# Moving two groups of tiles by 64 and 128 bytes within the 256-byte grid of on-chip memory

## The chip, the cores and the metric

The kernel runs on one core of one Trainium2 chip. The metric is the device time of one execution in microseconds (us). The profile is of one execution on the same kind of core. In it PE is TensorE's matmul, PEld is TensorE's loading of the stationary operand, DVE is VectorE, ACT is ScalarE, POOL is GpSimd and SP is SyncE. Both operands of a matmul lie in the on-chip memory, SBUF, which has 128 partitions; every tile here has one address, which is its byte offset in each of the partitions it spans.

## The reference

A decoder trunk for one sequence of 256 tokens and width 1024, in two layers. Each layer has two half-step SwiGLU feed-forward blocks (inner width 2816) around a mixer. The mixer of the first layer is a short gated convolution, that of the second is sparse attention (16 heads of 64) over one shared key and value set, which is projected from the stream between the layers.

```python
def rmsnorm(x, g):
    y = x * lax.rsqrt(jnp.mean(x * x, axis=-1, keepdims=True) + EPS)
    return y * g

def swiglu_ffn(x, w_in, w_out):
    gate, up = jnp.split(x @ w_in, 2, axis=-1)
    return (jax.nn.silu(gate) * up) @ w_out

def short_conv_mixer(x, w_in, conv_w, w_out):
    b_gate, c_gate, v = jnp.split(x @ w_in, 3, axis=-1)
    y = causal_depthwise_conv(c_gate * v, conv_w)        # width 3
    return (b_gate * y) @ w_out

for i in range(2):
    if i == 1:
        kv = shared_kv(h, ...)                           # x @ w_kv, compression, key norms
    h = h + 0.5 * swiglu_ffn(rmsnorm(h, ffn1_norm[i]), ffn1_w_in[i], ffn1_w_out[i])
    hn = rmsnorm(h, mix_norm[i])
    h = h + (short_conv_mixer(hn, ...) if i == 0 else nsa_mixer(hn, ..., kv))
    h = h + 0.5 * swiglu_ffn(rmsnorm(h, ffn2_norm[i]), ffn2_w_in[i], ffn2_w_out[i])
```

Almost all the arithmetic is in the matrix products with weights.

## The kernel before, in words

**Numbers in two halves.** TensorE multiplies here in a rounded 32-bit format. So that little is lost, each factor is split into a high part (the rounded value, written by ScalarE) and a low part (the remainder, written by VectorE). A product is high by high, low by high and high by low, three matmuls' worth of columns. An activation tile holds [high | low], 256 columns of each, 2048 bytes per partition. One matmul with the high weight as the stationary operand streams all 512 columns past it, and one with the low weight streams the 256 high columns. That is `half` (its matmul is the line that the profile calls L497), which the passes `a_pass`, `a_group`, `ffn_in` and `out_proj` call for nearly everything.

**Weights.** `W` brings weights from memory into staging tiles `ws` by SyncE's queue, ScalarE rounds them into `wh` (L260, L183), VectorE writes the remainder into `wl` (L288, L194); there are six buffers of 4096 bytes of each. `W.take` and `W.done` hand them to the matmuls in a fixed order and set how far ahead conversion may go. The order of instructions on each engine is written out by hand; no planner rearranges it.

**Pairs.** Three of the four feed-forward output projections go through `Blocks.product` (L843), within `inner_pairs` (about 131 to 181 us and 402 to 452 us) and the last one (about 900 to 955 us). There the hidden tiles are the stationary operand (128 columns of act, pr, hm, and a few of xs, kt or t2) and 512 columns of wh or wl stream past them. Other places where weights stream: the kv projection (L1085 to L1087, L1146) and the query projection `q_step` (L1420 to L1422, 256 columns, xs stationary). At L475, in the norm's row sums, the stationary tile is all ones.

**Where tiles lie.** `mk(shape, tag, bufs)` takes a tile from a pool in which each tag has `bufs` buffers of the size of its largest tile. The tags lie one behind the other in the order in which they are first used. In the kernel before, byte offsets in a partition are:

| tag | what | first address | buffers x bytes | address modulo 256 |
|---|---|---|---|---|
| ones | constant for the norm's sums | 640 | 1 | 128 |
| ws | staged weights | 29216 | 3 x 8192 | 32 |
| xs | normed activations | 53792 | 8 x 2048 | 32 |
| kt | attention keys, squares | 71200 | 1 x 8192 | 32 |
| wh, wl | high and low weights | 79392, 103968 | 6 x 4096 each | 32 |
| t2, t1 | temporaries | 128544, 142880 | 7 x 2048, 6 x 1024 | 32 |
| u | convolution input | 151072 | 2 x 1088 | 32 (the second 96) |
| act | hidden activations, high and low | 153248 | 22 x 2048 | 160 |
| pr, hm | hidden tiles of the pairs, attention's tiles | 198304, 216736 | 6 x 3072, 5 x 2048 | 160 |

Slices of these tiles that a matmul takes begin at multiples of 512 or 1024 bytes behind the tile's start, so a slice has the same address modulo 256 as its tile.

The tag "u" is first used in `Pairs.room`, whose tile of T + 16 = 272 numbers (T = 256) gives it 1088 bytes. Only T numbers of it are used there; the convolution (`conv_evac`) later takes tiles of T + 2.

Of the kernel before, what the change touches and what calls it, by code (L numbers as in the profile page):

```python
# [16 lines left out]
P = 128  # L17
T = 256
# [44 lines left out]
def trunk(ctx, tc, A, out):  # L63
# [9 lines left out]
    uid = [0]  # L73

    def mk(shape, tag, bufs, dt=F32, pool=None):
        uid[0] += 1
        return (pool or sb).tile(list(shape), dt, tag=tag, name=f"{tag}_{uid[0]}", bufs=bufs)
# [16 lines left out]
    def t1(shape=(P, T)):  # L94
        return mk(shape, "t1", 6)

    def sm(shape):
        return mk(shape, "sm", 24)


    class Halves:
        def __init__(self):
# [9 lines left out]
    class Stream:  # L112
# [110 lines left out]
        def room(self):  # L223
            i = len(self.units) + len(self.half)
            if i >= min(len(self.where), self.cap):
                return False
            return i in self.spare or i - sum(s < i for s in self.spare) < self.freed + self.limit
# [177 lines left out]
    def new_xs():  # L405
        return [mk([P, 512], "xs", 8, F32R) for _ in range(8)]
# [150 lines left out]
    class Pairs:  # L557
# [4 lines left out]
            self.homes, self.plain, self.f, self.left, self.both, self.n = homes, plain, [], [], None, 0  # L562

        def room(self):
            return mk([P, T + 16], "u", 2)[:, :T] if len(self.f) < 2 and 0 not in self.plain else t1()

        def parts(self, h, l, src):
            ac.copy(h, src)
# [151 lines left out]
        W.pump(1 if n == 8 else NBUF)  # L720


    xs = new_xs()
    nm = Norm([(xs, G_FFN1)])

    sq_all = mk([P, 4, 2, T], "kt", 1)
# [1126 lines left out]
```

## Time and profile before

| what | value |
|---|---|
| time, median of 3 runs | 963.18 us (962.69 to 963.33) |
| the profiled execution's own time | 962.88 us |
| its span, first to last instruction | 961.1 us |
| mean granted TensorE clock | 1.00 of full speed |
| busy: PE, PEld, DVE, ACT, POOL | 955.8, 827.2, 815.2, 618.0, 145.7 us |
| DMA read from memory | 175.52 MB, 184 GB/s over the span |

Busy times count an engine's instructions; PE and PEld overlap, and matmuls overlap each other in the pipeline, so a matmul's own duration (some 390 ns for 512 columns) is longer than the time from its start to the next one's. The group rows read: line, engine, operation, output <- inputs (the moving operand first or second, by name), sizes, count, then busy us and mean ns of one. Timeline rows read: start us, length us, engine, line, operation, output <- inputs, sizes, count of instructions that are run together in the row.

### The profile page before, as it was taken

The page shows a single profiled execution, that of the slowest core. Times are in us where ns is not written, and L with a number is a line of the kernel's source. Part 1 is how long each engine was busy: PE and PEld are TensorE (multiplying, and loading weights), DVE is VectorE, ACT ScalarE, POOL GpSimd, SP SyncE. Part 2 cuts the span into 40 slices and gives each one's busy share as a digit, 9 for nine tenths or more (in the row PEclk, how much of TensorE's full clock was granted, in tenths as well). Part 3 has the DMA queues.
Part 4 walks back from the last instruction along what each step waited for, and adds up shares of the span by engine and source line. Part 5 has one row for each costly group of instructions (what it writes and reads, how often), then busy time and mean ns, then how long its engine had stood idle before and what let it go on. Part 6 is the DMA issues. An engine that isn't in the chain of part 4 may idle for free.

```text
span 961.1 us, 14541 instructions
## 1 busy us (share of the span) xinstructions
PE 955.8 (99%) x5425; PEld 827.2 (86%) x5425; DVE 815.2 (85%) x1352; ACT 618.0 (64%) x1056; POOL 145.7 (15%) x231
## 2 busy tenths in 40 slices
PE   9999999999999999999999999999999999999998
PEld 7888888888888888888888898888987888888887
DVE  7898899898899888999968887865589788878996
ACT  7666665665556665666858777744589656656653
POOL 1000000024460000000021042002237350000002
PEclk9999999999999999999999999999999999999999
DMA  8665743464546567463536866554520354467361
GB/s 303 225 225 176 275 160 136 176 218 166 187 146 250 186 209 264 130 219 139 212 132 194 265 223 238 190 205 148 211 89 2 132 220 155 156 222 254 133 191 71
DMA packets 42150, 178.59 MB, mean 186 GB/s; under 512 B 3776, under 2 KB 7504, under 8 KB 27104
## 3 DMA queue, kind: packets, MB, share of 16 engines
q1 hardware_dynamic: 42080, 177.67, 54.1%
q8 instruction: 42, 0.69, 0.3%
q14 instruction: 28, 0.23, 0.1%
HBM read 175.52 MB, written 1.08 MB: 184 GB/s over the span
## 4 chain that ended last, share of the span: by engine, by line
PE 97%; DVE 1%; ACT 1%; DMA 0%; issue 0%
PE mm L497 55%; PE a L497 13%; PE a L843 12%; PE mm L843 6%; PE a L1146 1%; PE mm L750 1%; PE mm L1499 1%; PE a L1569 1%; PE a L1544 1%; PE a L789 1%; DVE pr L1507 0%; PE a L1239 0%; PE mm L752 0%; PE a L1085 0%; PE a L1087 0%; PE a L1086 0%
## 5 line engine op out<-in xcount | busy, mean ns | idle before, releaser
L497 PE MATMUL mm<-xs,wh 128*128 128x512 f32 x1480 | 349.0, 390 | 0.0
L497 PEld LDWEIGHTS mm<-xs,wh 128*128 128x128 f32 x1480 | 273.7, 188 | 54.4 <-DVE xs L452 0.2
L288 DVE TENSOR_TENSOR wl<-ws,wh 128x1024 fp32r<-128x1024 f32 x217 | 271.2, 1259 | 28.4 <-ACT wh L260 18.7
L260 ACT CAST wh<-ws 128x1024 fp32r<-128x1024 f32 x217 | 224.7, 1045 | 15.3 <-PE a L497 7.5
L497 PEld LDWEIGHTS mm<-xs,wl 128*128 128x128 f32 x1480 | 185.2, 191 | 4.2
L497 PE MATMUL mm<-xs,wl 128*128 128x256 f32 x1480 | 187.3, 283 | 0.0
L516 DVE TENSOR_TENSOR t<-mm,t 128x512 f32<-128x512 f32 x95 | 65.1, 685 | 37.8 <-ACT t L515 37.1
L515 ACT COPY t<-mm 128x512 f32<-128x512 f32 x95 | 55.4, 584 | 41.4 <-PE mm L497 40.9
L843 PE MATMUL a<-wh,act 128*128 128x512 f32 x286 | 78.2, 395 | 0.0
L843 PEld LDWEIGHTS a<-wh,act 128*128 128x128 f32 x286 | 53.7, 188 | 12.3
L540 ACT ACTIVATE t<-t 128x256 f32<-128x256 f32 x84 | 35.1, 418 | 43.7 <-DVE t L527 43.5
L497 PE MATMUL a<-act,wh 128*128 128x512 f32 x256 | 61.4, 395 | 0.0
L497 PEld LDWEIGHTS a<-act,wh 128*128 128x128 f32 x256 | 47.5, 188 | 10.6
L509 ACT CAST act<-t 128x256 fp32r<-128x256 f32 x77 | 31.3, 407 | 28.8 <-DVE t L966 18.5
L416 ACT ACTIVATE xs<-base 128x256 fp32r<-128x256 f32 x32 | 16.1, 508 | 50.4 <-DVE base L659 35.5
L527 DVE TENSOR_TENSOR t<-t,R 128x256 f32<-128x256 f32 (+1 forms) x88 | 45.0, 511 | 2.7
L194 DVE TENSOR_TENSOR wl<-base,wh 128x1024 fp32r<-128x1024 f32 x39 | 46.6, 1221 | 0.0
L843 PE MATMUL a<-wl,act 128*128 128x512 f32 x143 | 44.7, 394 | 0.0
L194 DVE TENSOR_TENSOR wl<-ws,wh 128x1024 fp32r<-128x1024 f32 x32 | 38.1, 1221 | 1.0 <-ACT wh L183 1.0
L541 DVE TENSOR_TENSOR t<-t,t 128x256 f32<-128x256 f32 x84 | 35.3, 420 | 2.9 <-ACT t L540 2.9
L510 DVE TENSOR_TENSOR act<-t,act 128x256 fp32r<-128x256 f32 x77 | 33.7, 438 | 4.3 <-ACT act L509 4.3
L183 ACT CAST wh<-base 128x1024 fp32r<-128x1024 f32 x32 | 32.5, 1044 | 6.7 <-DVE base L189 5.5
(379 smaller groups left out, 1435.5 us busy)
## 6 DMA issues: line engine op xcount, KB each, us to landing
ws<-in_ffn_w_in_dram SPq DMA_DIRECT2D x69, 1024.0 KB, 4.9
base<-in_ffn_w_pairs_dram SPq DMA_DIRECT2D x32, 512.0 KB, 5.2
ws<-in_ffn_w_pairs_dram SPq DMA_DIRECT2D x26, 512.0 KB, 4.8
ws<-in_conv_w_in_dram SPq DMA_DIRECT2D x12, 1024.0 KB, 4.8
ws<-in_ffn_w_out_dram SPq DMA_DIRECT2D x11, 1024.0 KB, 4.8
base<-in_ffn_w_in_dram SPq DMA_DIRECT2D x11, 1024.0 KB, 5.3
ws<-in_w_kv_dram SPq DMA_DIRECT2D x6, 1024.0 KB, 5.0
kt<-in_ffn_w_in_dram SPq DMA_DIRECT2D x5, 1024.0 KB, 8.3
```

The source lines that it names most:

```text
L183: ac.copy(h, src)
L194: ve.tensor_tensor(out=l, in0=src, in1=h.bitcast(F32), op=ALU.subtract)
L260: ac.copy(h, src)
L288: ve.tensor_tensor(out=l, in0=src, in1=h.bitcast(F32), op=ALU.subtract)
L497: pe.matmul(o if x == 0 else o[:, :T], u[x][:, q * P:(q + 1) * P], rhs if x == 0 else rhs[:, :T], start=start, stop=stop, skip_group_check ...
L510: ve.tensor_tensor(out=dst[:, T:], in0=src, in1=dst[:, :T].bitcast(F32), op=ALU.subtract)
L515: ac.copy(r, o[:, :, T:])
L516: ve.tensor_tensor(out=r, in0=o[:, :, :T], in1=r, op=ALU.add)
L527: ve.tensor_tensor(out=r, in0=r, in1=R[:, None, :].to_broadcast([P, n, T]), op=ALU.mult)
L540: ac.activation(s, r[:, 0], AF.Silu)
L541: ve.tensor_tensor(out=s, in0=s, in1=r[:, 1], op=ALU.mult)
L843: pe.matmul(self.m[n], x, w, start=(c == 0), stop=(c == 3 * self.total[n] - 1), skip_group_check=True)
```

## The change

A helper `gap(n)` takes a tile of n bytes that nothing uses, under a tag of its own. A gap of 64 bytes is taken just before the first xs tile, and one of 192 just after. The tag "u" grows from 1088 to 1152 bytes per buffer, of which there are two. No instruction is added, removed or reordered.

```diff
+    def gap(n):
+        mk([P, n // 4], f"gap{uid[0]}", 1)
...
         def room(self):
-            return mk([P, T + 16], "u", 2)[:, :T] if len(self.f) < 2 and 0 not in self.plain else t1()
+            return mk([P, T + 32], "u", 2)[:, :T] if len(self.f) < 2 and 0 not in self.plain else t1()
...
+    gap(64)
     xs = new_xs()
+    gap(192)
     nm = Norm([(xs, G_FFN1)])
```

By the table's sizes, xs comes to lie at 96 modulo 256; kt, wh, wl, t2, t1 and the first u stay at 32; and act, pr and hm come to lie at 32, since two times 1152 is a multiple of 256. 384 bytes per partition more are taken.

## The prediction

> **What bounds the kernel now.** I read the page first: the busy shares, the granted clock, the chain that ended last.
>
> ```profile
> span 961.1 us, 14541 instructions
> PE 955.8 (99%) x5425; PEld 827.2 (86%) x5425; DVE 815.2 (85%) x1352; ACT 618.0 (64%) x1056; POOL 145.7 (15%) x231
> PEclk9999999999999999999999999999999999999999
> PE 97%; DVE 1%; ACT 1%; DMA 0%; issue 0%
> L497 PE MATMUL mm<-xs,wh 128*128 128x512 f32 x1480 | 349.0, 390 | 0.0
> L497 PE MATMUL mm<-xs,wl 128*128 128x256 f32 x1480 | 187.3, 283 | 0.0
> L843 PE MATMUL a<-wh,act 128*128 128x512 f32 x286 | 78.2, 395 | 0.0
> ```
>
> TensorE is busy 99% of the span at full clock, and 97% of the chain is its own. No wait can be taken away, and the change adds no instruction. Only the time from one matmul's start to the next can move. A single matmul's mean (390 ns) is no measure of that, because matmuls overlap in the pipeline. I take the pace from the timeline instead: a run's start subtracted from the next run's start, divided by the run's count.
>
> **What the change moves.** Nothing but addresses. The weight tiles (wh, wl) and xs start at 32 modulo 256 before, and act, pr and hm at 160, because two convolution buffers of 1088 bytes make 2176, that is 8 x 256 + 128. Two of 1152 make 9 x 256, so act, pr and hm drop to 32, where weights lie. The 64 bytes ahead of xs put it at 96, and the 192 bytes behind it put the rest back at 32. Write "distance" for the start of the stationary operand less the start of the moving one, modulo 256. Three kinds of matmul change theirs: (a) act, pr or hm with wh or wl goes from 128 (half a turn) to 0; (b) xs moving through wh or wl goes from 0 to minus 64 (a quarter turn); (c) the few with xs as the stationary side, or xs beside pr and hm, get plus or minus 64.
>
> **Does the distance show in the trace?** Distance 0 first, xs moving through weights (start, length, count):
>
> ```profile
> 26.19 7.44 PE L497 MATMUL mm<-xs,wh 128*128 128x512 f32 x32
> 33.47 4.00 PE L497 MATMUL mm<-xs,wl 128*128 128x256 f32 x32
> 37.30 4.95 PE L497 MATMUL mm<-xs,wh 128*128 128x512 f32 x21
> ```
>
> (33.47 - 26.19) / 32 = 227.5 ns for 512 columns, and (37.30 - 33.47) / 32 = 119.7 ns for 256. Now half a turn, act moving through the same weights at the same line:
>
> ```profile
> 622.86 5.06 PE L497 MATMUL a<-act,wh 128*128 128x512 f32 x21
> 627.75 2.77 PE L497 MATMUL a<-act,wl 128*128 128x256 f32 x22
> 630.36 5.53 PE L497 MATMUL a<-act,wh 128*128 128x512 f32 x23
> 635.72 5.39 PE L497 MATMUL a<-act,wl 128*128 128x256 f32 x44
> 640.94 10.38 PE L497 MATMUL a<-act,wh 128*128 128x512 f32 x44
> 651.16 5.45 PE L497 MATMUL a<-act,wl 128*128 128x256 f32 x44
> 656.45 10.43 PE L497 MATMUL a<-act,wh 128*128 128x512 f32 x44
> ```
>
> 512 columns: 4.89/21 = 232.9, 5.36/23 = 233.0, 10.22/44 = 232.3. 256 columns: 2.61/22 = 118.6, 5.22/44 = 118.6, 5.29/44 = 120.2. So half a turn costs some 5.5 ns on 512 columns and saves up to 1 ns on 256. The same with weights as the moving side, at L843, half a turn:
>
> ```profile
> 139.63 2.03 PE L843 MATMUL a<-wh,act 128*128 128x512 f32 x8
> ...
> 146.61 0.62 PE L843 MATMUL a<-xs,pr 128*128 128x512 f32 x2
> ```
>
> 30 matmuls start between these rows: 6.98/30 = 232.7. With weights moving at distance 0 (the kv projection, its stationary side kt or t at 32):
>
> ```profile
> 477.81 0.39 PE L1086 MATMUL a<-wh,t 128*128 128x512 f32 x1
> ...
> 482.34 1.07 PE L497 MATMUL a<-kt,wh 128*128 128x512 f32 x4
> ```
>
> 20 matmuls, 4.53/20 = 226.5. It follows the distance and not the operand that moves: both orders give 227 at 0 and 232.5 at 128.
>
> **The cost of each part.** The counts:
>
> ```profile
> 0.00:961.10 961.10, 170.38 (x729) 137.19 (x729) 1.00 0.54 186
> L497 PE MATMUL a<-act,wh x256: 387/393/404, 255.8 to 770.3; 128*128 128x512 f32 x128
> L497 PE MATMUL mm<-act,wh x32: 387/393/476, 746.2 to 765.5; 128*128 128x512 f32 x32
> L497 PE MATMUL a<-xs,wh x56: 389/389/389, 204.0 to 255.6; 128*128 128x512 f32 x56
> L843 PE MATMUL a<-xs,hm x18: 390/393/404, 161.9 to 946.2; 128*128 128x512 f32 x18
> L843 PE MATMUL a<-xs,pr x15: 390/392/404, 146.6 to 917.6; 128*128 128x512 f32 x15
> L843 PE MATMUL a<-xs,act x3: 390/390/392, 169.8 to 945.9; 128*128 128x512 f32 x3
> L843 PE MATMUL a<-act,hm x6: 396/397/397, 132.7 to 404.2; 128*128 128x512 f32 x6
> ```
>
> (The first is the window view of L843 alone: 729 matmuls.)
> - L843 to distance 0: 729 less 36 with xs and 6 that keep their distance (act with hm) is 687; x (232.7 - 227.0) = minus 3.9 us.
> - L497, act moving, 512 columns: 288 x (232.7 - 227.5) = minus 1.5 us.
> - L497, act moving, 256 columns: 288 x (119.7 - 118.9) = plus 0.2 us (up to 0.3).
> - The attention's small matmuls on act, pr and hm: some 300, bounded by the same 6 ns, plus or minus 1.8 us; taken as nil, being of other widths with no pair of rows to compare.
> - The two gaps issue no instruction. Nothing is queued or waits: 0.
>
> Together minus 5.2, rounded down to 5.1 us, if VectorE and ScalarE keep up. This cover is thin where most of L843 stands:
>
> ```profile
> 131.00:181.00 50.00, 50.00 (x216) 40.50 (x215) 48.40 (x53) 32.38 (x43) 0.00 (x0) 1.00 0.48 168
> 402.50:452.00 49.50, 49.50 (x215) 40.12 (x214) 48.00 (x53) 32.37 (x43) 0.00 (x0) 1.00 0.50 170
> 901.00:947.00 46.00, 46.00 (x199) 37.29 (x199) 43.58 (x47) 29.45 (x38) 1.91 (x2) 1.00 0.48 160
> 24.00:127.00 103.00, 103.00 (x600) 91.45 (x599) 92.03 (x158) 67.63 (x106) 0.00 (x0) 1.00 0.65 220
> ```
>
> (PE busy, PEld, VectorE, ScalarE, POOL.) In the first window PE would need 216 x 5.7 = 1.2 us less: 48.8 us against VectorE's 48.4. It still fits, by 0.4.
>
> The Trainium skill speaks against all of this: "SBUF — State Buffer", section "Who interferes with whom", gives TensorE two independent read ports, one for the moving operand and one for LDWEIGHTS, and names the port pair of VectorE and GpSimd as the only contention. By that rule no address matters to a matmul, and the sum would be 0. The rows at 227.5 and 232.7 do not agree with it.
>
> **The large unknown is (b).** xs moving through weights is 1480 + 56 (L497) and 48 more (L750, L789) of each width: 1584 of 512 columns and 1584 of 256. No row has a stationary operand 64 below the moving one. Bounds:
> - Below: the pace at distance 0 has a part that does not grow with the columns. 227.5 - 119.7 = 107.8 ns for 256 columns, so 119.7 - 107.8 = 11.9 ns is fixed. Distance 128 leaves 118.6 - (232.7 - 118.6) = 4.5 by the same reckoning, so part of it depends on addresses. If a quarter turn removed all of it, 3168 x 11.9 = minus 37.7 us.
> - Above: half a turn's price, 1584 x 5.5 = plus 8.7 us. The dearest single row is longer: 404 ns at half a turn against 389 at distance 0, so 1584 x 15 = plus 23.8 us if every one were such.
>
> The nearest row of another distance than 0 and 128 is the norm's matmul, its stationary tile of ones at 128 against a moving t at 32 (plus 96):
>
> ```profile
> 487.00 1.07 PE L497 MATMUL a<-t,wh 128*128 128x512 f32 x4
> 487.91 1.07 PE L497 MATMUL a<-kt,wh 128*128 128x512 f32 x4
> 492.57 1.07 PE L497 MATMUL a<-t,wh 128*128 128x512 f32 x4
> 493.48 0.40 PE L475 MATMUL a<-t,ones 128*128 128x256 f32 x2
> ```
>
> The four ahead of it take 0.91/4 = 227.5 ns, as four with weights behind them do (0.91/4). So loading weights from another quarter shows neither gain nor loss. It is one load, and no steady stream of them. I take nil for (b), keep both ends for the range, and leave (c), under 230 matmuls, inside them.
>
> **The forecast.** The profiled execution took 962.9 us: 961.1 of span and 1.8 around it. 962.9 - 5.1 = 957.8. The median is 963.18, 0.3 above the profiled execution; from it the same gain gives 958.1. I say 958.
>
> **Rivals.**
> 1. *A quarter turn takes part of the fixed 11.9 ns.* For it: that part is left even where matmuls queue back to back, and half a turn changes it. Against it: the row of ones shows no gain. Half of it gives 19 us: 963.2 - 5.1 - 18.9 = 939. The Trainium skill bears on the floor: "TensorE: Matmul & The Clock Gate", section "Step-by-step: what each phase is for", says that loading the next tile's weights takes no read bandwidth from the running matmul; 512 columns at one per cycle of the 2.4 GHz it states would be 213.3 ns, an estimate, and the trace's 227.5 stays above it.
> 2. *A quarter turn costs like half a turn, or more: slower.* Its place is L497 with xs moving, over half of the span (1584 x 347 ns = 550 us). With 5.5 ns on each of 1584: 963.2 - 5.1 + 8.7 = 966.8; with 15 ns, 982. It decides from 5.1 us / 1584 = 3.2 ns per matmul of 512 columns. For it: the one other distance that the trace shows in a steady stream is dearer than 0, and VectorE's 92.03 of 103 us shows nothing else that could hold xs's stages. Against it: the row of ones.
> 3. *Addresses do not matter, or tiles do not land where the change's words say.* 963. It would need the 5.5 ns to belong to the stage rather than the distance. Against it: L497 shows both paces with the same weights, and L843 and L1086 both with weights moving. This is also what the first rule of the Trainium skill above would give.
> 4. *VectorE becomes the bound at L843.* With half the gain lost there and in the out-projections: minus 2 to 3 us, 960.5. For it: 48.40 of 50 us busy. Against it: 0.4 us of room.
>
> **How the numbers follow.** This kernel's runs tell a difference from none at about 0.2%, 1.9 us. Forecast 0.34; rival 1 0.24; rival 2 0.28; rival 3 0.08; rival 4 0.06. Faster: 0.34 + 0.24 + 0.04 of rival 4 = 0.62. Slower: 0.24 of rival 2. Same: the other 0.04 of rival 2 (near its break-even), 0.08 and 0.02 of rival 4 = 0.14. The likeliest case's own range is 955 to 960. Both signs hold much of the chance, so the whole range goes from 936 (rival 1 at a bit over half) to 972 (rival 2 with 9 ns on each).
>
> **What would show it.** In the changed kernel's rows, the medians of L497 with act moving fall from 393 to 389 ns, those of L843 from 392 to 389, and the 44-matmul runs from 10.22 to 10.0 us. The 32-matmul run of xs stays at 7.28 us if (b) is nil; 7.46 is rival 2, 7.1 or less rival 1. VectorE's busy time in 131 to 181 us stays at 48.4 while PE's stage shortens by 1.2 us; idle time of PE before L843, released by VectorE, would be rival 4. Paces of act unchanged at 232.7 would be rival 3 and break the sum. A span above 965 or below 950 would say that (b), taken as nil, was the larger term.

## The result, and the profile after

The changed kernel takes 955.56 us (median of 5 runs, 955.45 to 956.31) against 963.18 (962.69 to 963.33): a ratio of 0.9924, with a 95% interval of 0.9911 to 0.9938. That is 7.6 us faster, where 5.1 were forecast. One execution among the experiments below (all tiles 32 bytes on) took 1913.45 us at the full granted clock, twice as long as the others of its kernel, and is left out of that kernel's median. The changed kernel's profiled execution took 955.53 us, 953.7 of it span. From the page of the changed kernel:

```profile
span 953.7 us, 14541 instructions
PE 947.8 (99%) x5425; PEld 819.0 (86%) x5425; DVE 814.9 (85%) x1352; ACT 617.7 (65%) x1056; POOL 144.8 (15%) x231
PE 85%; DVE 9%; ACT 2%; issue 2%; POOL 1%; DMA 0%; SPq 0%; ACTq 0%; DVEq 0%
L500 PE MATMUL mm<-xs,wh 128*128 128x512 f32 x1480 | 351.2, 392 | 0.2 <-DVE xs L423 0.2
L500 PE MATMUL mm<-xs,wl 128*128 128x256 f32 x1480 | 181.4, 278 | 0.0
L848 PE MATMUL a<-wh,act 128*128 128x512 f32 x286 | 76.8, 391 | 0.0
```

The same instructions do the same work (L500 and L848 are the former L497 and L843). Three things differ. xs through 512 columns has a longer mean (390 to 392 ns), xs through 256 a shorter one (283 to 278), and L848 a shorter one (395 to 391). And the chain that ended last is no longer TensorE's alone: 9% of it is VectorE's, 2% ScalarE's. That share is no cost: the chain follows what came last, by however little, and TensorE is still busy 99% of the span.

The pace comes from the timeline of the changed kernel (start, length, count), first xs, then act:

```profile
33.23 3.93 PE L500 MATMUL mm<-xs,wl 128*128 128x256 f32 x32
37.00 7.49 PE L500 MATMUL mm<-xs,wh 128*128 128x512 f32 x32
44.33 3.93 PE L500 MATMUL mm<-xs,wl 128*128 128x256 f32 x32
48.10 7.49 PE L500 MATMUL mm<-xs,wh 128*128 128x512 f32 x32
55.42 3.79 PE L500 MATMUL mm<-xs,wl 128*128 128x256 f32 x32
59.05 5.20 PE L500 MATMUL mm<-xs,wh 128*128 128x512 f32 x22
...
636.87 10.16 PE L500 MATMUL a<-act,wh 128*128 128x512 f32 x44
646.88 5.44 PE L500 MATMUL a<-act,wl 128*128 128x256 f32 x44
652.15 10.16 PE L500 MATMUL a<-act,wh 128*128 128x512 f32 x44
```

xs through 512 columns: 7.33/32 = 229.1 ns and 7.32/32 = 228.8, up from 227.5. xs through 256 has two paces: 3.77/32 = 117.8 in the first two runs and 3.63/32 = 113.4 in the third, both below the 119.7 of before. act through 512: 10.01/44 = 227.5, down from 232.3; through 256: 5.27/44 = 119.8.

L848, the same 30 matmuls as in the prediction:

```profile
138.38 1.98 PE L848 MATMUL a<-wh,act 128*128 128x512 f32 x8
...
145.18 0.86 PE L848 MATMUL a<-xs,pr 128*128 128x512 f32 x3
```

6.80/30 = 226.7 ns, where it was 232.7.

**Where the 7.3 us of span between the two profiled executions come from.** Both programs issue the same matmuls in the same order, so the time from each one's start to the next can be subtracted one by one. Sums, in us; a difference of more than 28 ns on a single matmul, more than any pace explains, counts as a wait. The rows go by the moving operand, so those of xs and act take in the few at L848 that stream from these tiles:

```
kernel against before              changed    u alone   xs alone
xs through 512 columns               +2.0       -0.2       +2.1
xs through 256                       -6.4        0.0       -6.2
weights moving, 512 (L848 mostly)    -3.0       -3.7       +0.3
act through 512                      -1.4       -1.5        0.0
act through 256                      +0.2       +0.1        0.0
weights moving, 256 (queries)        -0.8        0.0       -1.1
waits                                +2.4       +1.2       +1.3
first 60 matmuls and the rest        -0.3       -0.1       +0.6
sum                                  -7.3       -4.2       -3.0
```

**The waits.** The changed kernel's view of what TensorE's weight loads waited for (us in total, times, longest); the same view of before has no wait at L843, and at L497 a single one of 0.2 us:

```profile
PEld mm L848 <- DVE wl L197: 1.0, 2, 0.5
PEld mm L500 <- DVE xs L423: 0.8, 2, 0.6
PEld mm L848 <- ACT wh L184: 0.6, 2, 0.4
PEld a L500 <- DVE act L513: 0.5, 1, 0.5
```

One place, in the timeline of the changed kernel, the loads and VectorE:

```profile
165.22 0.19 PEld L848 LDWEIGHTS mm<-wh,hm 128*128 128x128 f32 x1 [0.35 <-ACT wh L184]
...
166.47 0.30 PEld L848 LDWEIGHTS mm<-wl,hm 128*128 128x128 f32 x2 [0.50 <-DVE wl L197]
```

```profile
159.70 2.35 DVE L197 TENSOR_TENSOR wl<-base,wh 128x1024 fp32r<-128x1024 f32 x2
161.97 0.69 DVE L197 TENSOR_TENSOR xs<-ws,xs 128x512 fp32r<-128x512 f32 x1
162.57 2.67 DVE L192 TENSOR_TENSOR ws<-ws 128x1024 f32<-128x1024 f32 x3
165.20 2.46 DVE L197 TENSOR_TENSOR wl<-ws,wh 128x1024 fp32r<-128x1024 f32 x2
```

VectorE works without a gap here, and the low weights come when TensorE already stands. The matmul that follows (mm with wl and hm) started at 167.76 before and at 166.48 now, 1.28 us earlier; the 30 matmuls shown above had begun 1.25 us ahead of before (138.38 for 139.63) and ended 1.43 ahead. Of the 2.4 us of waits in the table, such places at L848 account for some 0.95. Most of the rest stands at L500, where VectorE wrote the normed xs (L423, about 277 to 281 us) or act (L513, about 255 us) too late.

### The profile page after: what moved, and what is told of

Read it like the earlier page. It is cut to its first block, busy times and chain, and to the rows that moved or that the text cites. A ratio compares the mean times of both kernels' runs of the same rounds, so it can differ in the third digit from the quotient of the medians.

```text
span 953.7 us, 14541 instructions
## 1 busy us (share of the span) xinstructions
PE 947.8 (99%) x5425; PEld 819.0 (86%) x5425; DVE 814.9 (85%) x1352; ACT 617.7 (65%) x1056; POOL 144.8 (15%) x231
## 4 chain that ended last, share of the span: by engine, by line
PE 85%; DVE 9%; ACT 2%; issue 2%; POOL 1%; DMA 0%; SPq 0%; ACTq 0%; DVEq 0%
PE mm L500 50%; PE a L848 11%; PE a L500 9%; PE mm L848 5%; DVE wl L291 3%; PE a L1151 1%; PE mm L1504 1%; PE a L1574 1%; PE mm L755 1%; ACT wh L263 1%; DVE wl L197 1%; PE a L1549 1%; DVE t L968 1%; PE a L794 1%; DMA base<-in_first_dram 0%
## 5 line engine op out<-in xcount | busy, mean ns | idle before, releaser
L500 PE MATMUL mm<-xs,wh 128*128 128x512 f32 x1480 | 351.2, 392 | 0.2 <-DVE xs L423 0.2
L500 PEld LDWEIGHTS mm<-xs,wh 128*128 128x128 f32 x1480 | 273.2, 188 | 56.8 <-DVE xs L423 0.8
L500 PEld LDWEIGHTS mm<-xs,wl 128*128 128x128 f32 x1480 | 179.5, 188 | 4.5
L500 PE MATMUL mm<-xs,wl 128*128 128x256 f32 x1480 | 181.4, 278 | 0.0
L848 PE MATMUL a<-wh,act 128*128 128x512 f32 x286 | 76.8, 391 | 0.0
L848 PEld LDWEIGHTS a<-wh,act 128*128 128x128 f32 x286 | 53.5, 188 | 11.2
L500 PE MATMUL a<-act,wh 128*128 128x512 f32 x256 | 60.5, 391 | 0.1
L500 PEld LDWEIGHTS a<-act,wh 128*128 128x128 f32 x256 | 47.4, 188 | 10.0 <-DVE act L513 0.5
L848 PE MATMUL a<-wl,act 128*128 128x512 f32 x143 | 44.0, 389 | 0.0
L513 DVE TENSOR_TENSOR act<-t,act 128x256 fp32r<-128x256 f32 x77 | 33.8, 439 | 4.3 <-ACT act L512 4.3
```

The costliest lines, as they stand in the source:

```text
L500: pe.matmul(o if x == 0 else o[:, :T], u[x][:, q * P:(q + 1) * P], rhs if x == 0 else rhs[:, :T], start=start, stop=stop, skip_group_check ...
L513: ve.tensor_tensor(out=dst[:, T:], in0=src, in1=dst[:, :T].bitcast(F32), op=ALU.subtract)
L848: pe.matmul(self.m[n], x, w, start=(c == 0), stop=(c == 3 * self.total[n] - 1), skip_group_check=True)
```

## The experiments

All were timed in 5 rounds or more beside the kernel before, whose median in the four groups was 962.65 to 962.85 us. The 512- and 256-column paces are read from 32-matmul runs of xs in the timeline, as above.

**u alone.** act, pr and hm moved, xs left at 32.

```diff
-    gap(64)
     xs = new_xs()
-    gap(192)
```

> Only the convolution's buffers at 1152 bytes, no gaps: act, pr and hm at 32, xs stays at 32 with the weights. Theory (the distance between the two operands' starts sets the pace, and the two edits add up): the forecast's part (a) alone, 963.2 - 5.1 = 958.1, up to 958.8 if some of it is lost to waits on VectorE; xs rows stay at 227.5 ns for 512 columns and 119.7 for 256, L843's run of 30 falls from 232.7 to 227. Rival (the whole gain is that of xs, act's part is lost to VectorE): 963. Rival (all of it is act's): 955.6.

Measured: 958.69 us, ratio 0.9956 (0.9944 to 0.9968). Timeline of this kernel:

```profile
33.41 4.00 PE L500 MATMUL mm<-xs,wl 128*128 128x256 f32 x32
37.24 7.44 PE L500 MATMUL mm<-xs,wh 128*128 128x512 f32 x32
44.52 4.00 PE L500 MATMUL mm<-xs,wl 128*128 128x256 f32 x32
```

xs keeps 119.7 and 227.5 ns. This is part (a) by itself: 4.2 us. By the table of sums the pace of the matmuls with act, pr and hm gave 5.1 (3.7 + 1.5 - 0.1), small groups another 0.3, and waits took 1.2 back.

The weights moving gave 3.7 us here and 3.0 in the changed kernel. The difference stands behind the few matmuls at L848 (L846 here) that have xs and pr, hm or act. There xs is the moving operand, not the stationary one: `second_home` lets some weights stay in xs buffers. The same place in the changed kernel and then with u alone:

```profile
145.18 0.86 PE L848 MATMUL a<-xs,pr 128*128 128x512 f32 x3
...
148.20 0.39 PE L848 MATMUL mm<-wl,pr 128*128 128x512 f32 x1
```

```profile
146.12 0.84 PE L846 MATMUL a<-xs,pr 128*128 128x512 f32 x3
...
149.07 0.39 PE L846 MATMUL mm<-wl,pr 128*128 128x512 f32 x1
```

13 matmuls start between the rows: 3.02/13 = 232.3 ns in the changed kernel, 2.95/13 = 226.9 with u alone. Only the three with xs have another distance in the changed kernel (minus 64, and 0 with u alone). The ten behind them are at distance 0 in both kernels, but in the changed one their single spacings are 234, 231, 233, 236, 224, 231, 236, 228, 233 and 231 ns before 226 to 227 comes back. So a matmul's spacing does not follow from its own distance alone; what ran before it counts too.

**xs alone.** The gaps, and the convolution's buffers as before.

```diff
-            return mk([P, T + 32], "u", 2)[:, :T] if ...
+            return mk([P, T + 16], "u", 2)[:, :T] if ...
```

> Only the gaps of 64 and 192, the convolution's buffers at 1088 as before: xs at 96, act, pr and hm stay at 160. Theory: xs through 256 columns goes from 119.8 to 115.7 ns and through 512 from 227.7 to 229.5 as in the changed kernel, 1584 x (1.8 - 4.1) = -3.6 us: 959.6; act's rows stay at 232.5. Rival (xs's quarter turn is worth nothing, as the forecast took it): 963.2.

Measured: 959.57 us, ratio 0.9965 (0.9951 to 0.9978), 3.3 us below before. The quarter turn of xs is worth something by itself, and in time the two parts add up: 4.2 + 3.3 = 7.5 of the 7.6.

**xs at 160, and weights at plus 64.** Gaps of 128 and 128, and in a second kernel 64 and 64.

```diff
-    gap(64)
+    gap(128)      # second kernel: gap(64), as in the changed kernel
     xs = new_xs()
-    gap(192)
+    gap(128)      # second kernel: gap(64)
```

The second kernel's expectation speaks of gaps of 192 and 64, which would put xs at 224. The kernel that ran has 64 and 64: xs stays at 96, and everything behind it (kt, wh, wl, t2, t1, u, act, pr, hm) moves on by 128, the weights to 160. The weights start 64 ahead of xs either way, so the distance is the plus 64 that was meant, and act, pr and hm keep distance 0 to the weights. It is called "plus 64" here; later expectations call it xs at 224.

> Gaps of 128 and 128, the rest as changed: xs at 160, half a turn from the weights; act, pr and hm at 32. Theory: xs gets half a turn's pace, 232.7 for 512 columns and about 119 for 256, so 1584 x (5.0 - 0.8) = +6.7 us over the kernel with u alone: about 965. Rival (any distance other than 0 does what the quarter turn does, or a gap's presence does it): 955.6. Rival (xs's place is of no weight): as with u alone, 958.

> Gaps of 192 and 64, the rest as changed: xs at 224, so the weights' start is 64 ahead of it rather than 64 behind. Theory with only the size of the distance counting: as changed, 955.6 within 0.7. Rival (the sign counts, since the load of the next weights starts some 3 ns after the matmul and runs slower than it, 128 columns in 188 ns): another pace for 512 and 256 columns, anywhere from 950 to 966, and the two 256-column paces of 113 and 118 ns of the changed kernel do not both come back.

Measured: 965.15 us for xs at 160 (ratio 1.0024, 1.0014 to 1.0033) and 957.70 for plus 64 (0.9947, 0.9934 to 0.9959). Timelines, 160 and then plus 64:

```profile
37.88 7.63 PE L500 MATMUL mm<-xs,wh 128*128 128x512 f32 x32
45.34 3.95 PE L500 MATMUL mm<-xs,wl 128*128 128x256 f32 x32
49.14 7.63 PE L500 MATMUL mm<-xs,wh 128*128 128x512 f32 x32
```

```profile
37.03 7.63 PE L500 MATMUL mm<-xs,wh 128*128 128x512 f32 x32
44.50 3.80 PE L500 MATMUL mm<-xs,wl 128*128 128x256 f32 x32
48.14 7.62 PE L500 MATMUL mm<-xs,wh 128*128 128x512 f32 x32
```

160 gives half a turn's pace, 7.46/32 = 233.1 and 3.80/32 = 118.8 ns: the same gaps in other sizes make the kernel slower than before. Plus 64 gives 233.4 and 113.8. So the sign counts: the weights 64 ahead of xs cost 4 ns more on 512 columns than 64 behind it, and 256 columns take the lower of the two paces in nearly every run.

**xs at 64, at 128.** Gaps of 32 and 224, and of 96 and 160.

```diff
-    gap(64)
+    gap(32)       # second kernel: gap(96)
     xs = new_xs()
-    gap(192)
+    gap(224)      # second kernel: gap(160)
```

> Gaps of 32 and 224, the rest as changed: xs at 64, 32 from the weights. Theory names no number for -32; if the pace changes smoothly with the distance, between 0 and -64: 227.9 to 229.2 ns and 119.7 to 115.6, so 956 to 959. Rival (memory lines of 64 bytes count, and 32 splits them): slower than with u alone, above 960.

> Gaps of 96 and 160, the rest as changed: xs at 128, 96 from the weights. Between -64 and half a turn if smooth: 229.2 to 233.1 ns for 512 and 115.6 to 118.7 for 256, 956 to 965. Rival (lines of 64 bytes): like -32 or slower.

Measured: 962.01 us (0.9994, 0.9986 to 1.0003) and 966.69 (1.0043, 1.0031 to 1.0056). Timelines, 64 and then 128:

```profile
37.13 7.63 PE L500 MATMUL mm<-xs,wh 128*128 128x512 f32 x32
44.60 3.90 PE L500 MATMUL mm<-xs,wl 128*128 128x256 f32 x32
48.33 7.63 PE L500 MATMUL mm<-xs,wh 128*128 128x512 f32 x32
```

```profile
37.90 7.63 PE L500 MATMUL mm<-xs,wh 128*128 128x512 f32 x32
45.37 4.00 PE L500 MATMUL mm<-xs,wl 128*128 128x256 f32 x32
49.21 7.63 PE L500 MATMUL mm<-xs,wh 128*128 128x512 f32 x32
```

The pace isn't smooth in the distance, so the smooth guess failed in both. At -32 and at -96 512 columns take 233.4 ns, as at half a turn; 256 take 116.6 and 120.0. Of the distances tried, 512 columns are quick only at 0 and -64.

**256 bytes more.** u alone, and a gap of 256 behind xs.

```diff
-    gap(64)
     xs = new_xs()
-    gap(192)
+    gap(256)
```

> As with u alone, plus a gap of 256 bytes behind xs: every distance between xs and the weights grows by 256, none modulo 256, and as many bytes are used as in the changed kernel. Theory (only the distance modulo 256 counts): as with u alone, 958.7 within 0.5, paces 227.9 and 119.7. Rival (the distance counts modulo 512 or more, or absolute addresses do): another time, and other paces for xs.

Measured: 958.72 us (0.9959, 0.9945 to 0.9972), as with u alone; its 32-matmul runs stand at the same 7.28 and 3.83 us. Bytes taken, and a whole 256 of distance, change nothing.

**All tiles 32 bytes on.** u alone, and the changed kernel, with a gap of 32 ahead of the first tile of the pool (the constants, ones among them, lie in another pool and stay).

```diff
         mk([P, n // 4], f"gap{uid[0]}", 1)
+
+    gap(32)
```

> As with u alone, plus a gap of 32 bytes ahead of the first tile: ws, xs, kt, wh, wl, t2, t1, act, pr and hm all move from 32 to 64, every distance stays. Theory (the distance between the operands alone sets the pace): 958.7 within 0.5, 227.9 and 119.7 ns. Rival (starts that are multiples of 64 bytes save a step of the 6.67 ns of which the steady paces 226.7, 120.0 and 113.3 are multiples, since an operand then covers one piece of 64 bytes less): 6.67 ns less on each of some 3170 xs matmuls, 21 us, and as much less on act's: 935 or below.

> The changed kernel, plus a gap of 32 bytes ahead of the first tile: xs at 128, weights and all else at 64, every distance as in the changed kernel. Theory: 955.6 within 0.5, with the two paces 113.3 and 117.7 ns for 256 columns. Rival (the place within 64 bytes counts): as for the run before, about 20 us less.

Measured: 958.80 us (0.9959, 0.9946 to 0.9972) and 955.32 (0.9922, 0.9910 to 0.9934). Both are as without the 32 bytes. xs at 128 with weights at 64 is as quick as xs at 96 with weights at 32, while xs at 128 with weights at 32 is the slowest kernel here. Of the two places within 64 bytes that were tried, 0 and 32, neither is quicker; the distance has weight.

**wl moved instead of xs.** If each matmul has the pace of its own two operands, 512 columns (with wh) can stay at distance 0 and 256 (with wl) can go to another. u alone, and gaps around the first wl:

```diff
-        w = [[mk([P, 2, 4, P], t, NBUF, F32R) for t in ("wh", "wl")] for _ in range(4)]
+        def weights(n):
+            t = mk([P, 2, 4, P], "wh", NBUF, F32R)
+            if n == 0:
+                gap(64)       # second kernel: 192; third: 128
+            l = mk([P, 2, 4, P], "wl", NBUF, F32R)
+            if n == 0:
+                gap(192)      # second kernel: 64; third: 128
+            return [t, l]
+
+        w = [weights(n) for n in range(4)]
```

> As with u alone, and the low weights moved instead of xs: 64 bytes between the wh and wl tags and 192 behind wl, so wl at 96, all else at 32. Theory (the pace belongs to the pair of operands of each matmul): the 512-column matmuls of xs and act stay at distance 0 (227.9 ns), the 256-column ones get +64 and the 114.0 ns that xs at 224 showed, 1872 x (119.7 - 114.0) = -10.7 us; wl as the moving side at L843 gets -64 and 229.2 ns, 240 x 1.8 = +0.4; from 958.7 that gives 948.4, up to 951 if VectorE holds some of it up. Rival (512- and 256-column pace are tied, since runs of both alternate and a lower pace of one is paid back by the other as in the changed kernel): no lower than 955.

Measured: 956.90 us (0.9940, 0.9928 to 0.9953). Timeline of this kernel:

```profile
36.89 7.44 PE L500 MATMUL mm<-xs,wh 128*128 128x512 f32 x32
44.17 3.93 PE L500 MATMUL mm<-xs,wl 128*128 128x256 f32 x32
47.94 7.44 PE L500 MATMUL mm<-xs,wh 128*128 128x512 f32 x32
```

512 columns stay at 227.5 as planned, but 256 take 3.77/32 = 117.8, not the 113.8 of plus 64, though the distance is the same. The distance allows both, as minus 64 already did in the changed kernel, so something else takes part; the entry into the run is where to look. So the 948.4 fell, and with it the theory that a distance has one pace.

What differs at the entry is seen in single spacings (ns) at the end of a 512-column run and the start of the next 256-column run, the bar between them:

```
changed kernel   226 229 232 226 229 232 | 113 113 114 113 113 114
changed kernel   229 232 226 229 232 226 229 | 120 117 118 118 118 117
plus 64          231 236 231 235 231 236 | 118 114 113 113 114 113
wl at 96         227 226 227 227 226 227 226 | 118 118 117 118 118 118
```

With the changed kernel the 512-column pace goes in threes, 226, 229, 232. A run that ends on the 232 is followed by 113.3 ns, one that ends on the 229 by 120 and then 117.7. Runs of 32 end on one and the other by turns (32 isn't a multiple of 3), but for the few behind a wait; the convolution's two runs of 48 are both followed by 113.3.

The second and third kernel of this edit ask whether a given entry always gives the same pace: wl at 224 with xs at 32, and the changed kernel with wl at 160.

> As with u alone, and wl at 224 (gap of 192 ahead of wl, 64 behind): 512 columns of xs and act at distance 0, their 256 columns at -64; wl as the moving side of L843 at +64, 240 x (233 - 227) = +1.4 us. Theory (a distance has several steady paces, and the phase at which a run is entered picks one): from the steady 226.7 the 256-column runs all take the same one; 113.3 ns gives 1872 x (113.3 - 119.7) = -12.0, 948.1; 117.7 gives -3.7, 956.4, as with wl at 96. Rival (the mean of the changed kernel, 115.6, belongs to the distance): -7.7, 952.4.

> The changed kernel, and wl at 160 (gaps of 128 around it): 512 columns of xs at -64 as in the changed kernel, their 256 columns at +64; wl at L843 at half a turn, 240 x 5.4 = +1.3 us. Theory as above: if both phases in which the 512-column runs end lead to 113.3 ns at this distance, 1584 x (113.4 - 115.6) = -3.5 and 955.5 + 1.3 - 3.5 = 953.3; if the runs are still of two kinds, 956.9; if all of them take 117.7, 1584 x 2.1 = +3.3, 960.

Measured: 957.91 us (0.9950, 0.9937 to 0.9962) and 955.92 (0.9931, 0.9917 to 0.9944). Timelines, wl at 224 and then xs at 96 with wl at 160:

```profile
36.85 7.46 PE L500 MATMUL mm<-xs,wh 128*128 128x512 f32 x32
44.15 3.93 PE L500 MATMUL mm<-xs,wl 128*128 128x256 f32 x32
47.92 7.46 PE L500 MATMUL mm<-xs,wh 128*128 128x512 f32 x32
```

```profile
32.99 3.79 PE L500 MATMUL mm<-xs,wl 128*128 128x256 f32 x32
36.62 7.49 PE L500 MATMUL mm<-xs,wh 128*128 128x512 f32 x32
43.95 3.96 PE L500 MATMUL mm<-xs,wl 128*128 128x256 f32 x32
47.75 7.49 PE L500 MATMUL mm<-xs,wh 128*128 128x512 f32 x32
```

In the first, 3.77/32 = 117.8 again, in this and the other runs, though the distance is the changed kernel's: behind a steady 227 the 256 columns took the upper pace in every run of both kernels with wl moved from u alone. The time is 1.5 us above the 956.4 worked out for it: xs through 512 columns lost 0.7 against u alone (7.30/32 = 228.1, since the first nine or so of each run take 224 to 236 ns, as behind xs at L848), and the weights moving lost 2.7 where 1.4 had been counted. In the second, both kinds are back, 3.63/32 = 113.4 and 3.80/32 = 118.8; the mean over xs's 256 columns is 114.8, against 115.6 in the changed kernel, but L848 with wl moving gave back what that won (-1.4 us for weights moving in place of -3.0). Neither kernel beats the changed one, and the only one below it, the changed kernel with all tiles 32 bytes on, is within the noise of it.

Mean spacing by distance (stationary start less moving start, modulo 256) over all matmuls with xs moving through weights, in ns, spacings of over 290 and 150 left out as waits. The rows are from the kernels that leave wl with wh; with wl at 96 and at 224, 256 columns at plus and minus 64 take 117.7 and 117.6:

```
distance          0    -32    -64    -96    128    +64
512 columns   227.9  233.3  229.1  233.3  233.1  233.2
256 columns   119.7  116.7  115.6  120.0  118.7  114.0
```

## Why the prediction was right, and where it was not

- **What bounds the kernel.** Right: no wait was taken away, and pace moved the time.
- **Part (a), act, pr and hm to distance 0.** Right. Forecast minus 3.9, minus 1.5 and plus 0.2; measured with u alone minus 3.7, minus 1.5 and plus 0.1. In the changed kernel it came to minus 3.0, minus 1.4 and plus 0.2, for the reason given under (c). The 30 matmuls at L848 went from 232.7 to 226.7 ns, as the kv projection's 226.5 had said.
- **Part (b), xs to minus 64, taken as nil.** This step failed. It gave plus 2.0 us on 512 columns and minus 6.4 on 256, net minus 4.4 in pace, and 3.3 in time by itself. The step that misled was the nearest row: one load of the ones tile at plus 96 showed nothing, but a steady stream at minus 96 takes 233.4 ns, 6 more than at 0 (plus 96 itself was not run, and the sign counts). One load within another rhythm doesn't measure a distance. The bounds were sound: rival 1 (a quarter turn takes part of the fixed 11.9 ns) happened for 256 columns, 119.7 to 115.6, a third of it; the price of rival 2 happened, smaller, for 512. The sign that was to tell them apart, the run of 32 at 512 columns (7.28 us for nil, 7.46 for rival 2, 7.1 for rival 1), came out at 7.33: it watched the width that lost and not the one that won.
- **Part (c), the few others, left without a price.** Two groups show. The query projection with xs stationary won 0.8 us. The few matmuls at L848 that stream xs through pr, hm and act cost some 0.7, on the ten or so matmuls at distance 0 behind each group of them; a count of the matmuls that change their distance does not find these.
- **The cover.** The prediction found 0.4 us of room on VectorE at the first L843 stage and took the gain in full. Waits took back 2.4 us in the changed kernel and 1.2 with u alone. The sum of busy times over 50 us hid that VectorE is late at single points, where several conversions stand in a row: with u alone nearly all of the 1.2 us is at the two L846 stages before 500 us. So rival 4's mechanism happened beside the forecast, at half its price with u alone. In the changed kernel the waits reach its price, but more than half of them lie outside L848, where TensorE caught up with VectorE's writes of xs and act; with xs alone the same places wait (1.3 us in all), and none at L848.
- **Rival 2** (a quarter turn costs like half a turn) fell for minus 64. It describes plus 64, minus 32 and minus 96 on 512 columns. Its higher case, 15 ns, was nowhere: the dearest mean is 5.4 above distance 0.
- **Rival 3** (addresses do not matter) fell: with the weights at 0, minus 32, minus 64, minus 96, 128 and plus 64 from xs, and act, pr and hm at 0 from the weights in all six, the time was 958.7, 962.0, 955.6, 966.7, 965.2 and 957.7 us. The rule named beside it, from the Trainium skill's "SBUF — State Buffer", section "Who interferes with whom", that TensorE's two read ports are independent, does not agree with these six if it is read as the prediction reads it, that no address matters to a matmul.

That 958 came near 955.6 is partly luck. Of the 7.3 us between the profiled executions, part (a) made 4.2 (5.1 forecast); the missed 4.4 + 0.8 us of gain and the missed 2.4 us of waits have opposite signs.

The runs do not show what in the chip makes the pace depend on the distance. They show that the distance counts, and that 32 bytes more on both sides, or 256 more between them, do not. In a steady stream a matmul's own stationary operand and the next one's, whose load runs beside it, lie at the same place modulo 256, so the runs do not tell which of the two counts. Why minus 64 and plus 64 differ also stays open. How the run before ended goes with the pace that is taken, but no run set that end by itself, so that it decides is likely and not shown.

## What to carry to other kernels

Where TensorE is 99% busy and loads new weights for each matmul, read the time from one matmul's start to the next by pair of operands, and try where one operand's tiles start modulo 256 against the other's: here the best and the worst of six distances differ by 11 us in 960, at no instruction. Choose by measuring, not by analogy, since neighbours 32 bytes apart differ by 2 to 11 us and a few single matmuls in the old trace say nothing. Count also what a few matmuls at another distance do to those behind them. And before counting a faster pace in full, look at single points where the engine that feeds it works without a gap: an average of 97% busy left 0.4 us on paper, and each of the two such stages cost 0.4 to 0.6.

## What the runs showed of the hardware that had not been expected

- Spacing of matmuls that queue back to back settles into fixed rhythms: 226.7 ns at distance 0, a group of 226, 229, 232 at minus 64, and for 256 columns 120.0, 117.7 or 113.3. Behind another rhythm the 226.7 comes back only after nine or ten matmuls of 224 to 236.
- At one distance more than one rhythm is stable (113.3 and 117.7 at minus 64 and at plus 64), and how the run before ended goes with which is taken.
- The sign of the distance counts: 229.1 against 233.2 ns for 512 columns at minus and plus 64.
